# A hybrid SSD and attention encoder: dt in the exponents, a beginning in written order, and the gated norm chunk by chunk with its channel weights in the output weights

## Chip, cores and metric

The kernel runs on one core of one Trainium2 chip (the chip has eight). The metric is the device time of one execution in microseconds, the median of several runs. The core has a tensor engine (PE; its weight loads are PEld), a vector engine (DVE), a scalar engine (ACT), GpSimd (POOL) and a queue engine (SP); each goes through its own instructions in order and waits on semaphores of the others.

## What is computed

Two layers on x of 512 tokens by 1024 channels, then a final norm. Of a layer, shortened:

```python
h = rms_norm(x, norm1_w[i]); proj = h @ w_in[i]
z, xbc, dt_raw, q, k, v = split(proj)
xs, bm, cm = split(silu(depthwise_conv7(xbc)))
dt = softplus(dt_raw + dt_bias[i]); a = -exp(a_log[i])
y = ssd(xs, dt_fwd, a_fwd, bm, cm) + flip(ssd(flip(xs), flip(dt_bwd), ...)) + d_skip[i] * xs
y_ssm = rms_norm(y * silu(z), ssm_norm_w[i])     # per group of 512 channels
y_attn = windowed_gqa(q, k, v, sink, bias)       # |i-j| <= 128
x = x + concat(y_ssm, y_attn) @ w_out[i]
h = rms_norm(x, norm2_w[i]); g, u = split(h @ w_up[i])
x = x + (silu(depthwise_conv3(g)) * u) @ w_down[i]
```

ssd works in chunks of 128 tokens. Inside a chunk the output is a product with the matrix (C B^T) * exp(cum[l] - cum[s]) * dt[s], for s <= l forward and s >= l backward; across chunks a state is passed on, with 16 heads of 64 channels in two groups of eight heads.

## The kernel before

Everything is one program of some 20,000 instructions, four token tiles of 128 rows. A scheduler of the framework orders the instructions of each engine by priority and estimated times; the side work below is spread by hand.

**Weights.** Each product with weights is made in three parts: a block of weights is loaded raw by SP (prep_raw, L140), ACT casts it to a high part (whi, L152) and DVE subtracts to get the low part (wlo, L153, both in prep_split). mm3 (L263 to L265) then makes the three products with the activations, which are split the same way. Three raw and three split blocks are in flight.

**Beginning.** load_x0 (L226) loads the token tiles in halves, norm_weight (L216) loads the norm weight broadcast to 128 rows (512 KB). norm_token makes two Squares with a row sum on ACT (L287), the reciprocal root on POOL (L289, L290), one half of the product with the weight on DVE (L299) and the other on ACT and POOL (L301, L302); eight 128-column transposes on PE follow (L310), then a cast to the high part on ACT (L313) and the low part on DVE (L314). The bias table of attention is made by one product (L418), written to DRAM and spread into four Toeplitz arrays. The first product with weights is vdt: v and dt of all tokens, 96 products over 288 columns in layer 0. Then setup makes 42 small transposes of channel parameters (L256), dt_step makes softplus by a series on DVE (L483 to L498), six cumulative sums on PE (L511), their Exp on ACT (ex, L512), copies of the running sums (run, L515), their transposes (L518) and the write to DRAM (sums).

**State-space part.** Per group, bc_turn makes C B^T per chunk and two masked copies of it on DVE, cbf and cbb. ssd_steps returns a list of steps that Side.run spreads over the products with weights: over z (g_z) for the first group, over the output product (g_out) for the second. A unit u is four heads of a chunk, eight units per group. fetch loads the running sums as rows (POOL queue), build makes cbf * dt_fwd on ACT (L817) and adds cbb * dt_bwd on DVE (L818), decay subtracts each token's own sum on DVE (L828), takes the minimum of the two directions (L832), Exp on ACT (L833) and the product with build's result (L834, em). inner multiplies em with x on PE (L843). states passes the chunk states on (L785 to L794), outer adds the part from the states and d_skip * x (L855 to L866), multiplies by silu(z) and sums squares on ACT (L867).

**Gated norm.** After the last chunk, scale makes one reciprocal root for all four chunks (L274) and scales each on ACT (L873). turn then transposes by channel block j, all four chunks (L883), and applies the channel weight nprm in the cast (ACT, L884) and in the low part (DVE, L885). The output product reads mixS: group 0 in the last two weight blocks of each half (o0, o1), group 1 in token_outer (o2).

## Time and profile before

| | us |
|---|---|
| three runs: lowest, median, highest | 1574.24, 1574.35, 1574.81 |
| the profiled execution | 1572.24 |
| its span, first to last instruction | 1570.5 |
| PE busy / weight loads / DVE / ACT / POOL | 1518.9 / 1242.4 / 936.9 / 780.1 / 186.3 |
| mean granted clock of PE | 0.993 |

The rows further down come from one profiled execution. A row of a timeline has the start from the span's first instruction, the length, engine, line, operation, written and read tile, count, and in brackets the idle time before with what ended it. A row of a group has the count, the busy time, the mean of one in ns, and the idle time of the engine ahead of it. Tile names are the program's; many tiles share the name t (split activations) or pd and psm (PSUM banks).

### The profile page before, as it was taken

What the parts mean: (1) busy time and instruction counts of PE and PEld (TensorE: products, weight loads), DVE (VectorE), ACT (ScalarE), POOL (GpSimd) and SP (SyncE); (2) the same over time, 40 slices, a digit from 0 to 9 for tenths busy, and PEclk for the clock granted to TensorE, in tenths of its full rate; (3) what the DMA queues carried; (4) which work ended last, traced back from release to release, by engine and by line L of the source; (5) the groups of instructions that cost most, each with busy time, mean ns of one, the idle gap of its engine ahead of it and who ended that gap; (6) DMA issues with size and microseconds to landing.
All of it is one profiled execution on the core that took longest, in us unless ns stands there. A gap on an engine that the chain in (4) does not pass through costs nothing.

```text
span 1570.5 us, 20117 instructions
## 1 busy us (share of the span) xinstructions
PE 1518.9 (97%) x7676; PEld 1242.4 (79%) x7676; DVE 936.9 (60%) x1494; ACT 780.1 (50%) x1378; POOL 186.3 (12%) x226
## 2 busy tenths in 40 slices
PE   5999999999999999999999999989999999999997
PEld 5887778878788888888788777877778888888886
DVE  3776778996544444433367677799946444444333
ACT  4577886752543233322355789877335323332223
POOL 4000003433200000000010000043322000000002
PEclk9999999999999999999999999999999999999999
DMA  8432333553233333333343222336422323333221
GB/s 248 116 88 77 92 94 95 149 148 90 80 98 95 106 96 95 94 95 94 97 135 113 77 75 74 95 97 186 123 93 81 94 94 99 103 94 94 94 94 67
DMA packets 113796, 162.00 MB, mean 103 GB/s; under 512 B 8010, under 2 KB 90186, under 8 KB 113692
## 3 DMA queue, kind: packets, MB, share of 16 engines
q1 hardware_dynamic: 105476, 133.12, 27.8%
q0 software_dynamic: 7648, 27.50, 7.0%
q8 instruction: 60, 0.98, 0.3%
q14 instruction: 36, 0.29, 0.1%
q10 hardware_dynamic: 576, 0.10, 0.0%
HBM read 156.34 MB, written 8.55 MB: 105 GB/s over the span
## 4 chain that ended last, share of the span: by engine, by line
PE 81%; DVE 9%; issue 3%; ACT 3%; POOL 2%; DMA 1%; POOLq 0%; DVEq 0%; ACTq 0%
PE pd L263 21%; PE pd L264 20%; PE pd L265 20%; PE psm L263 3%; PE psm L264 3%; PE psm L265 3%; PE psm L608 2%; PE psm L598 2%; DVE dd L818 2%; DVE wlo L153 2%; PE psm L564 1%; ACT whi L152 1%; PE psm L565 1%; DVE rows L828 1%; PE psm L843 1%
## 5 line engine op out<-in xcount | busy, mean ns | idle before, releaser
L153 DVE TENSOR_TENSOR wlo<-raw,whi 128x1024 fp32r<-128x1024 f32 (+1 forms) x230 | 282.1, 1230 | 267.6 <-ACT whi L152 266.2
L263 PE MATMUL pd<-t,whi 128*128 128x512 f32 (+1 forms) x1088 | 419.0, 386 | 0.0
L265 PE MATMUL pd<-t,wlo 128*128 128x512 f32 (+1 forms) x1088 | 418.6, 385 | 0.4 <-DVE wlo L153 0.4
L264 PE MATMUL pd<-t,whi 128*128 128x512 f32 (+1 forms) x1088 | 418.0, 384 | 0.0
L152 ACT CAST whi<-raw 128x1024 fp32r<-128x1024 f32 (+1 forms) x230 | 238.5, 1041 | 263.9 <-PE pd L264 207.1
L265 PEld LDWEIGHTS pd<-t,wlo 128*128 128x128 f32 x1088 | 204.4, 188 | 40.3 <-DVE wlo L153 1.6
L263 PEld LDWEIGHTS pd<-t,whi 128*128 128x128 f32 x1088 | 204.2, 188 | 39.7 <-issue 1.9
L264 PEld LDWEIGHTS pd<-t,whi 128*128 128x128 f32 x1088 | 204.5, 188 | 39.1 <-issue 1.5
L263 PE MATMUL pd<-whi,t 128*128 128x256 f32 (+2 forms) x544 | 190.9, 351 | 0.6 <-ACT t L884 0.5
L264 PE MATMUL pd<-wlo,t 128*128 128x256 f32 (+2 forms) x544 | 182.8, 336 | 0.4 <-DVE wlo L153 0.2
L265 PE MATMUL pd<-whi,t 128*128 128x256 f32 (+2 forms) x544 | 181.8, 335 | 0.0
L263 PEld LDWEIGHTS pd<-whi,t 128*128 128x128 f32 x544 | 106.2, 195 | 13.7 <-issue 3.3
L264 PEld LDWEIGHTS pd<-wlo,t 128*128 128x128 f32 x544 | 106.2, 195 | 13.3 <-issue 3.8
L265 PEld LDWEIGHTS pd<-whi,t 128*128 128x128 f32 x544 | 105.6, 194 | 9.5 <-issue 0.6
L1026 DVE TENSOR_TENSOR pl<-t,ph 128x512 fp32r<-128x512 f32 x40 | 27.7, 692 | 119.4 <-ACT ph L1025 119.4
L1025 ACT CAST ph<-t 128x512 fp32r<-128x512 f32 x40 | 24.8, 620 | 147.7 <-PE psm L264 137.2
L360 DVE SCALAR_TENSOR_TENSOR sg<-pd,fprm,sg 128x511 f32<-128x511 f32 x88 | 65.9, 749 | 30.7 <-ACT sg L354 29.0
L566 DVE CUSTOM_DVE_ANT_0 s<-psm,bias,sink_all 128x256 f32<-128x256 f32 (+1 forms) x128 | 65.5, 548 | 22.8 <-PE psm L565 10.3
L580 ACT ACTIVATE s<-s,nm 128x257 f32<-128x257 f32 (+1 forms) x128 | 70.6, 556 | 2.6 <-DVE nm L577 2.5
L360 DVE SCALAR_TENSOR_TENSOR xT<-pd,cprm,xT 128x511 f32<-128x511 f32 (+2 forms) x96 | 66.9, 743 | 5.8 <-ACT xT L354 3.8
L263 PE MATMUL pd<-whi,ph 128*128 128x512 f32 x176 | 69.7, 396 | 0.0
L264 PE MATMUL pd<-wlo,ph 128*128 128x512 f32 x176 | 69.6, 396 | 0.0
(186 smaller groups left out, 2210.0 us busy)
## 6 DMA issues: line engine op xcount, KB each, us to landing
raw<-in_w_up_dram SPq DMA_DIRECT2D x88, 512.0 KB, 3.5
raw<-in_w_in_dram SPq DMA_DIRECT2D x52, 512.0 KB, 4.0
raw<-in_w_down_dram SPq DMA_DIRECT2D x44, 512.0 KB, 3.5
rows<-sums POOLq DMA_DIRECT2D x32, 512.0 KB, 5.7
raw<-in_w_out_dram SPq DMA_DIRECT2D x32, 512.0 KB, 4.2
bias<-toep POOLq DMA_DIRECT2D x16, 384.0 KB, 3.8
raw<-in_w_in_dram SPq DMA_DIRECT2D x18, 256.0 KB, 3.4
toep<-table POOLq DMA_DIRECT2D x4, 1024.0 KB, 9.5
```

The costliest lines, as they stand in the source:

```text
L152: S.copy(hi[:, :used], raw[:, :used])
L153: V.tensor_tensor(lo[:, :used], raw[:, :used], f(hi[:, :used]), ALU.subtract)
L263: mm(o, lh, rh, start=start, stop=False)
L264: mm(o, lh, rl, start=False, stop=False)
L265: mm(o, ll, rh, start=False, stop=stop)
L360: V.scalar_tensor_tensor(dst[:, lo:hi], src[:, lo + d : hi + d], taps[k], dst[:, lo:hi], ALU.mult, ALU.add)
L566: V.tensor_tensor_reduce(out=s4[:, h, :w], in0=ps[:, :w], in1=it.bias[h // 2][:, h % 2, it.j0 : it.j1], scale=1.0, scalar=sink4[:, h : h + 1],
L580: S.activation(s4[:, h, : w + 1], s4[:, h, : w + 1], AF.Exp, bias=nm4[:, h : h + 1], accum_out=den[:, h : h + 1])
L598: turn128(ps[:, c : c + P], it.s4[:, h, b * P : (b + 1) * P], ident)
L608: mm(po[c * HD : (c + 1) * HD, :256], v_sb[:, it.k0 // P + b, it.g * HD : (it.g + 1) * HD], it.pts[b][:, c * 256 : (c + 1) * 256], start=( ...
L818: V.scalar_tensor_tensor(dd[:, hs], cbb[:, cs], dts[:, c, 16 + hh + h : 17 + hh + h], dd[:, hs], ALU.mult, ALU.add)
L1026: V.tensor_tensor(l, p_sb[kt], f(h), ALU.subtract)
```

## The change

Four things. (1) dt goes into the exponents: dt_step makes ln(dt) with one Newton step after Ln and Exp, and own = ln(dt) - running sum; decay adds own of the backward direction on ACT (Identity with bias), copies it over the forward rows where the mask says s > l (a predicated copy on DVE), takes Exp with own of the forward direction as bias on ACT, and multiplies by the unmasked C B^T. build and the masked copies go; the backward direction's diagonal goes into skf, the factor of x in outer. (2) In layer 0 everything up to the end of vdt is in written order; the norm weight comes as one row of 4 KB and is spread by two products with ones; each token tile is one transfer, its norm one Square and two DVE products; the bias table comes behind the first vdt products. (3) The gated norm gets a reciprocal root per chunk, DVE scales the chunk, and turn transposes a chunk's four channel blocks. (4) The channel weights go into the split of those w_out blocks that multiply the state-space channels.

```diff
-            S.copy(hi[:, :used], raw[:, :used])
-            V.tensor_tensor(lo[:, :used], raw[:, :used], f(hi[:, :used]), ALU.subtract)
+            if key in scaled:
...
+                n = used // len(scaled[key])
+                for k, col in enumerate(scaled[key]):
+                    ks, wcol = slice(k * n, (k + 1) * n), nprm[:, col, key[0] : key[0] + 1]
+                    S.activation(hi[:, ks], raw[:, ks], AF.Copy, scale=wcol)
+                    V.scalar_tensor_tensor(lo[:, ks], raw[:, ks], wcol, f(hi[:, ks]), ALU.mult, ALU.subtract)
+            else:
+                S.copy(hi[:, :used], raw[:, :used])
+                V.tensor_tensor(lo[:, :used], raw[:, :used], f(hi[:, :used]), ALU.subtract)
...
                 add_unit((i, f"o{half}", j), wo, kt0, 2, [(512 * half, 512)])
+                if j >= 4:
+                    scaled[i, f"o{half}", j] = (kt0, kt0 + 1)
         for j in range(4):
             add_unit((i, "o2", j), wo, 4 + j, 1, [(0, 1024)])
+            scaled[i, "o2", j] = (4 + j,)
...
+    start = ExitStack()
+    start.enter_context(tc.manual_schedule())
...
-    load_x0(0)
-    wb0 = norm_weight(npool0, norm1_w[0])
+    wrow = npool0.tile([1, D], F32, name="wrow")
+    nc.scalar.dma_start(wrow, norm1_w[0:1])
+    nc.sync.dma_start(x_sb[0], x_in[0:P])
     prep_raw(1)
-    load_x0(1)
+    nc.sync.dma_start(x_sb[1], x_in[P : 2 * P])
...
+    wb0 = npool0.tile([P, D], F32, name="wb0")
+    for b in range(2):
+        psw = small_bank()
+        mm(psw, ones[0:1], wrow[:, 512 * b : 512 * b + 512], start=True, stop=True)
+        V.tensor_copy(wb0[:, 512 * b : 512 * b + 512], psw)
...
+    def first_norm(t):
+        xn = npool0.tile([P, D], F32, tag="xn", name=nm("xn"), bufs=2)
+        ss = smp.tile([P, 1], F32, tag="ss1", name=nm("ss"))
+        S.activation(xn, x_sb[t], AF.Square, scale=1.0 / 32.0, accum_out=ss)
+        rs = smp.tile([P, 1], F32, tag="rs1", name=nm("rs"))
+        G.tensor_scalar(rs, ss, EPS, None, ALU.add)
+        G.tensor_tensor(rs, rs, mhalf, ALU.pow)
+        yield
+        for b in range(2):
+            cs = slice(512 * b, 512 * b + 512)
+            V.scalar_tensor_tensor(xn[:, cs], x_sb[t][:, cs], rs, wb0[:, cs], ALU.mult, ALU.mult)
+        yield
+        for b in range(2):
+            turn_split(xn, t, b, hT)
+        yield
+    def turn_split(xn, t, b, dst):
...
+            if i == 0:
+                norms = [first_norm(t) for t in range(NT)]
+                next(norms[0])
+                next(norms[0])
+                prep_split(1)
+                next(norms[0])
+                next(norms[1])
+                next(norms[1])
+                prep_split(2)
+                next(norms[1])
+                next(norms[2])
+                next(norms[2])
+                prep_split(3)
+                vw = [splits.pop((i, "vdt", j)) for j in range(3)]
+                vdt(0, 0)
+                vdt(1, 0)
+                vdt(0, 1)
+                next(norms[2])
+                next(norms[3])
+                next(norms[3])
+                vdt(1, 1)
+                vdt(0, 2)
+                vdt(1, 2)
+                prep_raw(WBUF + RBUF)
+                bias_table()
+                next(norms[3])
+                for t in (2, 3):
+                    for j in range(3):
+                        vdt(t, j)
+                S.activation(expa_all, alog_all, AF.Exp)
+                start.close()
+            else:
+                vw = [take((i, "vdt", j)) for j in range(3)]
+                for t, j in ((t, j) for t in range(NT) for j in range(3)):
+                    vdt(t, j)
...
+                V.tensor_scalar(sp_w, dts, 1e-37, None, ALU.max)
+                S.activation(sp_a, sp_w, AF.Ln)
+                S.activation(sp_w2, sp_a, AF.Exp, scale=-1.0)
+                V.tensor_tensor(sp_w, sp_w, sp_w2, ALU.mult)
+                V.scalar_tensor_tensor(sp_a, sp_w, -1.0, sp_a, ALU.add, ALU.add)
...
+                V.tensor_tensor(
+                    own.rearrange("p c d h -> p c (d h)"), sp_a, run.rearrange("p c d h -> p c (d h)"), ALU.subtract
+                )
+                V.tensor_tensor(own[:, :, 1], own[:, :, 1], own[:, :, 0], ALU.subtract)
...
-                    cbf = ep.tile([P, L], F32, tag="cbf", name=nm("cbf"), bufs=2)
-                    cbb = ep.tile([P, L], F32, tag="cbb", name=nm("cbb"), bufs=2)
+                    cb = ep.tile([P, L], F32, tag="cb", name=nm("cb"), bufs=2)
...
-                    pv = ps.rearrange("p (c l) -> p c l", c=NT)
-                    for dst, m in ((cbf, t_le), (cbb, t_ge)):
-                        V.tensor_tensor(
-                            dst.rearrange("p (c l) -> p c l", c=NT),
-                            pv,
-                            f(m).unsqueeze(1).broadcast_to([P, NT, P]),
-                            ALU.mult,
+                    S.copy(cb, ps)
...
+                        V.scalar_tensor_tensor(
+                            junk, ps[:, sl], 1.0, ident, ALU.mult, ALU.mult, accum_out=own_cb[:, c : c + 1]
                         )
-                    r.update(bk=bk, cbf=cbf, cbb=cbb)
+                    skf = ep.tile([P, NT, GH], F32, tag="skf", name=nm("skf"), bufs=2)
+                    V.tensor_tensor(skf, dts[:, :, 16 + GH * g : 16 + GH * g + GH], bc_last(own_cb, GH), ALU.mult)
...
-                def build(u):
-                    c, hh = u // 2, h0 + 4 * (u % 2)
-                    dd = s2("dd", 3)
-                    cs = slice(c * P, (c + 1) * P)
-                    for h in range(4):
-                        hs = slice(h * P, (h + 1) * P)
-                        S.mul(dd[:, hs], cbf[:, cs], dts[:, c, hh + h : hh + h + 1])
-                        V.scalar_tensor_tensor(
-                            dd[:, hs], cbb[:, cs], dts[:, c, 16 + hh + h : 17 + hh + h], dd[:, hs], ALU.mult, ALU.add
-                        )
-                    dcb[u] = dd
-
                 def decay(u):
-
-
                     c, hh = u // 2, h0 + 4 * (u % 2)
                     rw = rows.pop(u)
+                    for h in range(4):
+                        S.activation(rw[:, 1, h], rw[:, 1, h], AF.Identity, bias=own[:, c, 1, hh + h : hh + h + 1])
+                    V.copy_predicated(rw[:, 0], behind.unsqueeze(1).broadcast_to([P, 4, P]), rw[:, 1])
+                    for h in range(4):
+                        S.activation(rw[:, 0, h], rw[:, 0, h], AF.Exp, bias=own[:, c, 0, hh + h : hh + h + 1])
+                    em = s2("em", 3)
                     V.tensor_tensor(
-                        rw, rw, run[:, c, :, hh : hh + 4].unsqueeze(3).broadcast_to([P, 2, 4, P]), ALU.subtract
+                        v4(em), rw[:, 0], cb[:, c * P : (c + 1) * P].unsqueeze(1).broadcast_to([P, 4, P]), ALU.mult
                     )
-                    em = s2("em", 3)
-                    V.tensor_tensor(v4(em), rw[:, 0], rw[:, 1], ALU.min)
-                    S.activation(em, em, AF.Exp)
-                    V.tensor_tensor(em, em, dcb[u], ALU.mult)
                     ems[u] = em
...
-                    G.tensor_tensor(v3(y), v3(xk[:, c]), bc_last(skip_all[:, 16 * i + h0 : 16 * i + h0 + GH], HD), ALU.mult)
+                    G.tensor_tensor(v3(y), v3(xk[:, c]), bc_last(skf[:, c], HD), ALU.mult)
...
-                    S.activation(y, sz[:, c], AF.Square, accum_out=ss[:, c : c + 1])
-
-                def scale():
-                    rs = rstd_of(ss, 512, NT)
+                    ss = smp.tile([P, 1], F32, tag="gss", name=nm("gss"))
+                    S.activation(y, sz[:, c], AF.Square, accum_out=ss)
+                    rss[c] = rstd_of(ss, 512)
+                rss = {}
+                def turn(c):
                     sz = r["sz"]
-                    for c in range(NT):
-                        S.mul(sz[:, c], sz[:, c], rs[:, c : c + 1])
-                    mixS[g] = (act_tile(), act_tile())
-
-                def turn(js):
-                    oh_, ol_ = mixS[g]
-                    sz = r["sz"]
-                    for j in js:
-                        wcol = nprm[:, 4 * g + j, i : i + 1]
-                        ps = small_bank()
-                        for c in range(NT):
-                            turn128(ps[:, c * P : (c + 1) * P], sz[:, c, j * P : (j + 1) * P], ident)
-                        S.activation(oh_[:, j], ps, AF.Copy, scale=wcol)
-                        V.scalar_tensor_tensor(ol_[:, j], ps, wcol, f(oh_[:, j]), ALU.mult, ALU.subtract)
+                    if mixS[g] is None:
+                        mixS[g] = (act_tile(), act_tile())
+                    V.tensor_scalar(sz[:, c], sz[:, c], rss[c], None, ALU.mult)
+                    ps = small_bank()
+                    pv = ps.rearrange("p (k c) -> p k c", k=4)
+                    for j in range(4):
+                        turn128(pv[:, j], sz[:, c, j * P : (j + 1) * P], ident)
+                    h, l = (m[:, :, c * P : (c + 1) * P] for m in mixS[g])
+                    S.copy(h, pv)
+                    V.tensor_tensor(l, pv, f(h), ALU.subtract)
...
-                    if k in range(8):
-                        build(k)
-
-                steps = [lambda k=k: step(k) for k in range(-1, 10)]
-                steps.append(scale)
-                steps += [lambda: turn((0, 1)), lambda: turn((2, 3))]
-                return steps
+                return [lambda k=k: step(k) for k in range(-1, 10)] + [lambda c=c: turn(c) for c in range(NT)]
```

The order of PE in layer 0 after vdt. Before, the small transposes (ident, with crow, frow, nrow) and the sums of dt (sp_e with the triangles) stand among products of the next projection (pd_678):

```order
L265 MATMUL pd_678<-t_9_116,wlo_600 128x512
L263 MATMUL pd_678<-t_9_116,whi_599 128x512
L256 MATMUL psm_460<-ident,nrow 128x2 x8
L511 MATMUL psm_493<-sp_e_471,t_le 128x64
L511 MATMUL psm_493<-sp_e_471,t_gt 128x64
L511 MATMUL psm_493<-sp_e_471,t_ge 128x64
L511 MATMUL psm_493<-sp_e_471,t_lt 128x64
L511 MATMUL psm_493<-sp_e_471,ones 128x64 x2
L264 MATMUL pd_678<-t_10_117,whi_599 128x512
L265 MATMUL pd_678<-t_9_116,wlo_600 128x512
L263 MATMUL pd_678<-t_9_116,whi_599 128x512
```

In the change the same stretch, from the last products of vdt (pd_190) to the first of the k projection (pd_514):

```order
L279 MATMUL pd_190<-wlo_252,t_12_123 128x288
L280 MATMUL pd_190<-whi_251,t_13_124 128x288
L271 MATMUL psm_409<-ident,crow 128x16 x12
L271 MATMUL psm_423<-ident,frow 128x8 x22
L271 MATMUL psm_447<-ident,nrow 128x2 x8
L581 MATMUL psm_481<-sp_e_459,t_le 128x64
L581 MATMUL psm_481<-sp_e_459,t_gt 128x64
L581 MATMUL psm_481<-sp_e_459,t_ge 128x64
L581 MATMUL psm_481<-sp_e_459,t_lt 128x64
L581 MATMUL psm_481<-sp_e_459,ones 128x64 x2
L278 MATMUL pd_514<-t_10_121,whi_516 128x512
L599 MATMUL psm_498<-ident,run_185 32x128 x4
```

The transposes, the sums and the running sums' transposes now follow vdt directly, and the next projection comes after them.

The order of ACT at the same place in the change; whi_516 is the high part of the first weight block of the k projection:

```order
L505 COPY v_177<-pd_190 128x256
L537 ACTIVATE expa_all<-alog_all 128x64
L554 ACTIVATE sp_e_459<-sp_e_459 128x128
L586 ACT_TABLE_LOAD
L586 ACTIVATE sp_a_462<-sp_w_460 128x128
L587 ACT_TABLE_LOAD
L587 ACTIVATE sp_w_60_461<-sp_a_462 128x128
L582 ACTIVATE ex_180<-psm_481 128x384
L161 CAST whi_516<-raw_329 128x1024
L592 COPY run_185<-psm_481 128x4x16 x2
L161 CAST whi_520<-raw_331 128x1024
```

That split now stands behind Ln, two Exps and two table loads; before, three splits stood ahead of the Exp of sp_e.

The order of DVE in the first group's state-space stretch of layer 0. Before, some one and a half units:

```order
L828 TENSOR_TENSOR rows_2605<-rows_2605,run_276 128x1024
L864 TENSOR_TENSOR y_2715<-y_2715,psm_2621 128x512
L832 TENSOR_TENSOR em_2742<-rows_2605 128x512
L866 TENSOR_TENSOR t_459_2389<-t_459_2389,y_2715 128x512
L818 SCALAR_TENSOR_TENSOR dd_2746<-cbb_859,dts_277,dd_2746 128x128 x4
L828 TENSOR_TENSOR rows_2690<-rows_2690,run_276 128x1024
L834 TENSOR_TENSOR em_2742<-em_2742,dd_2725 128x512
L832 TENSOR_TENSOR em_2825<-rows_2690 128x512
```

In the change, a like piece:

```order
L875 TENSOR_TENSOR xf_4501<-t_424_2171,sd_181 128x512
L939 TENSOR_TENSOR yo_2735<-psm_2733,ex_180 128x512
L911 TENSOR_TENSOR em_2729<-rows_2531,cb_864 128x512
L907 COPY_PREDICATED rows_2618<-t_gt,rows_2618 128x512
L941 TENSOR_TENSOR y_2731<-y_2731,psm_2634 128x512
L907 COPY_PREDICATED rows_2700<-t_gt,rows_2700 128x512
L943 TENSOR_TENSOR t_470_2414<-t_470_2414,y_2731 128x512
L911 TENSOR_TENSOR em_2762<-rows_2618,cb_864 128x512
```

Of a unit there remain a predicated copy and one product.

## Rows read from the trace of the kernel before

**Rows 1.** Page, its head: span, then busy time per engine with share and instructions.

```profile
span 1570.5 us, 20117 instructions
PE 1518.9 (97%) x7676; PEld 1242.4 (79%) x7676; DVE 936.9 (60%) x1494; ACT 780.1 (50%) x1378; POOL 186.3 (12%) x226
```

**Rows 2.** Stretches: length, busy us of PE, PEld, DVE, ACT, POOL; clock; DMA share; GB/s.

```profile
246.08:307.08 61.00, 56.25 (x378) 48.30 (x377) 58.98 (x87) 44.58 (x85) 27.68 (x22) 0.94 0.52 123
307.08:322.00 14.92, 13.88 (x67) 10.81 (x65) 14.75 (x21) 9.35 (x15) 6.16 (x5) 1.00 0.73 250
...
394.70:401.10 6.40, 3.24 (x17) 2.39 (x16) 1.93 (x3) 4.25 (x7) 1.23 (x2) 0.84 0.28 91
1017.70:1077.10 59.40, 53.34 (x361) 46.91 (x359) 58.06 (x83) 44.16 (x79) 24.02 (x22) 0.94 0.44 117
1165.30:1171.40 6.10, 2.63 (x18) 1.71 (x17) 1.97 (x3) 4.29 (x7) 1.23 (x2) 1.00 0.31 113
...
920.00:960.00 40.00, 40.00 (x237) 30.48 (x236) 29.61 (x79) 37.28 (x81) 3.80 (x9) 1.00 0.28 79
```

**Rows 3.** Waits of PE: line and its releaser; total us, times, longest.

```profile
PE psm L883 <- ACT t L873: 7.9, 11, 2.1
PE psm L843 <- DVE em L834: 7.3, 6, 1.7
```

**Rows 4.** Groups by line and shape, 246 to 307 us, ACT, then DVE.

```profile
L817 ACT ACTIVATE dd<-cbf,dts 128x128 f32<-128x128 f32 x41 | 13.3, 391 | 5.9 <-DVE em L834 5.9
L152 ACT CAST whi<-raw 128x1024 fp32r<-128x1024 f32 x7 | 7.3, 1039 | 2.2 <-PE pd L265 2.2
L833 ACT ACT_TABLE_LOAD x5 | 6.4, 1283 | 0.1
L833 ACT ACTIVATE em<-em 128x512 f32<-128x512 f32 x8 | 5.1, 632 | 7.4 <-DVE em L832 7.4
...
L818 DVE SCALAR_TENSOR_TENSOR dd<-cbb,dts,dd 128x128 f32<-128x128 f32 x34 | 16.8, 541 | 0.0
L828 DVE TENSOR_TENSOR rows<-rows,run 128x1024 f32<-128x1024 f32 x8 | 10.6, 1323 | 0.0
L153 DVE TENSOR_TENSOR wlo<-raw,whi 128x1024 fp32r<-128x1024 f32 x7 | 8.5, 1217 | 0.6 <-ACT whi L152 0.6
L832 DVE TENSOR_TENSOR em<-rows 128x512 f32<-128x512 f32 x8 | 7.4, 923 | 0.0
```

**Rows 5.** Timeline of PE, 0 to 40 us: start, length, instruction, idle before.

```profile
10.96 1.88 PE L418 MATMUL psm<-oh,rb 32*32 32x512 f32 x2 [10.96 <-DMA oh<-in_onehot_dram]
15.53 1.11 PE L310 MATMUL psm<-ident,xn 128*128 128x128 f32 x4 [2.69 <-DVE xn L299]
...
22.34 0.59 PE L263 MATMUL pd<-whi,t 128*128 128x288 f32 x1
...
39.22 0.40 PE L263 MATMUL pd<-t,whi 128*128 128x512 f32 x1
```

**Rows 6.** Timeline, 0 to 26 us: ACT, POOL, DVE.

```profile
6.18 0.63 ACT L287 ACTIVATE xn<-x 128x512 f32<-128x512 f32 x1 [0.26 <-DMA x<-in_x_dram]
21.57 2.04 ACT L313 CAST t<-psm 128x512 fp32r<-128x512 f32 x4
...
14.12 1.10 POOL L290 TENSOR_TENSOR rs<-rs,mhalf 128x1 f32<-128x1 f32 x2
...
14.72 1.41 DVE L299 SCALAR_TENSOR_TENSOR xn<-x,rs,wb 128x512 f32<-128x512 f32 x2 [1.21 <-POOL rs L290]
```

**Rows 7.** DVE timeline, 42 to 49 us; then PE busy in lines L256 and L511.

```profile
42.18 0.18 DVE L472 TENSOR_TENSOR xdt<-pd,dtb_all 128x32 f32<-128x32 f32 x1
48.16 0.29 DVE L498 SCALAR_TENSOR_TENSOR sp_e<-dts,expa_all 128x128 f32<-128x128 f32 x1
...
39.00:76.00 37.00, 3.09 (x42) 2.82 (x42) 1.00 0.42 113
...
39.00:76.00 37.00, 1.55 (x12) 1.41 (x12) 1.00 0.42 113
```

71 lines of the change are left out of this document (39 added, 32 removed).

## The prediction

> **What bounds the kernel now.** I read the head of the page first: the span is 1570.5 us and PE is busy for 97% of it [rows 1], so a change pays only where PE waits, or where it runs at the lower clock because it has just waited. The page leaves 51.6 us of the span in which PE is not busy. The table of stretches says where they lie. In the first head group's state-space stretch (from the first state product to the last inner product) PE is busy 56.25 of 61.00 us in layer 0 and 53.34 of 59.40 us in layer 1, and the granted clock is 0.94 in both (a mean over the two levels, 2.4 and 1.2 GHz: it falls to the lower one after a wait). Where the gated norm of the second group is turned, PE is busy 3.24 of 6.40 us and 2.63 of 6.10 us [rows 2]. The table of waits names the releasers: the turn L883 waits 7.9 us for the ACT scaling L873, and the inner product L843 waits 7.3 us for the DVE product L834 [rows 3]. The rest is the beginning: the first transpose starts at 15.53 us and the first product with weights at 22.34 us [rows 5].
>
> In the state-space stretch DVE is the engine that ends last: busy 58.98 of 61.00 us, against 44.58 us for ACT [rows 2]. Of it the combined mask products (L818) are 16.8 us, the subtraction over 1024 columns (L828) 10.6 us and the minimum (L832) 7.4 us [rows 4].
>
> **State-space stretch, first group.** Per unit (eight per group) the change takes from DVE four L818, one L828 and one L832, and adds one predicated copy over 512 columns. From ACT it takes four L817 and the 512-column Exp, and adds eight ACTIVATEs over 128 columns. DVE loses 16.8 + 10.6 + 7.4 = 34.8 us. The predicated copy is nowhere in this trace: at least the 512-column L832 (0.92 us), at most the 1024-column L828 (1.32 us), since it writes half as much; I take 0.92, as the width is the same. Eight of them and four rescalings of about 0.8 us leave DVE at 58.98 - 34.8 + 7.4 + 3 = 35 us. It no longer binds. ACT: 13.3 us for 41 L817 is 0.324 each, so 64 x 0.324 = 20.8 us come and 32 x 0.324 + 5.1 = 15.5 us go, and ACT has 44.6 + 5.3 = 49.9 us [rows 4]. What PE itself needs is 61.00 less 4.75 idle and less what the clock cost (6% of 61.00 = 3.7 us): 52.6 us; in layer 1 it is 59.40 - 6.06 - 3.6 = 49.7 us [rows 2]. So ACT, with 49.9 us and every step in order, is now as full as PE. A unit crosses ACT, DVE, ACT, DVE instead of DVE, ACT, DVE, and in the change's order some of its Exps stand behind a Silu that waits for PE, while two DVE products stand behind a sum from POOL. At most 8.4 and 9.7 us can come back, at least nothing. I take a little over half: 4.5 and 5.0 us, together **-9.5 us**.
>
> **Gated norm by chunk.** Now four ACT scalings follow one rstd over all four chunks, and no turn can start before them. The change scales a chunk on DVE as soon as its own rstd is there, and the order puts the first group's turns between blocks of 24 products. That stretch, 14.92 us long, has 1.04 us idle, and the four scalings make PE wait between the turns too; I take 1.5 us a layer, bounds 0 and 2. In the second group PE still turns all 16 in one piece after 24 products, but only the last chunk can be late. PE idles 3.16 and 3.47 us there now, and its clock is 0.84 in layer 0 [rows 2]. I take 3.7 us a layer, bounds 2 and 4.5, since the last chunk's chain of DVE, POOL and ACT is no longer than those 24 products and the first 12 transposes; late next is the split of the next weight block, on DVE before the turned chunks. Together **-3.0 and -7.4 us**.
>
> **The channel weights** move into the split of eight weight blocks a layer. Four become two ACTIVATEs and two DVE operations over 512 columns: some 0.3 us more on either engine each. The rest keep their sizes. In those stretches ACT and DVE have slack once the mask work is gone, so I cost it at nothing; without that cover it would be 8 x 0.3 = 2.4 us. The single-chunk rstds add three pairs on POOL per group, hidden beside its 27.68 busy of 61.00 us [rows 2].
>
> **Attention stage.** DVE loses two masked products per group and gains four 128-column ones and two small ones, about even. ACT gains one 512-column copy per group, four in all at 0.6 us. In layer 1 ACT is busy 37.28 of 40.00 us there [rows 2]. Between 0 and 2.4 us; I take **+0.8 us**.
>
> **The beginning.** Now the first token tile is normalized only after 512 KB of broadcast norm weight, on ACT, POOL and DVE with two POOL products; PE's first weight product starts at 22.34 us and the 96 of them end where the next projection begins, at 39.22 us: 16.9 us, with 16 transposes among them [rows 5]. In the change the tiles run one behind the other, since ACT makes a tile's two casts before the next tile's Square. One tile is: Square 1.2 us, rstd 0.9 (half of the pair's 1.10 and its sum before), DVE 0.7 + 0.7, second turn 1.1 at the low clock, cast 0.5 [rows 5, 6]: 5.1 us. Tile 0 can start at 6.2, where the second half of it is read now [rows 6]. The weight row has then to go through two products like L418 (1.88 us) and two copies, which holds tile 0 back by about a microsecond, and tile 1 is turned at about 17.1 us. From there PE has the same 96 products and 16 transposes as now, 16.9 us, and the bias product of 0.9 us: it is through at 35 us instead of 39.2. That is **-4.2 us**; bounds 0 (late tiles 2 and 3) and 6 us. SP issues the four tiles as one transfer each and no longer has blocks of the next projection, which wait for buffers, ahead of the last one. POOL sends out the bias table and the four Toeplitz writes later than now; what reads them comes only with the attention stage, so I cost that at nothing, and a first attention step that waited for them would cost PE a few us.
>
> **What stands behind it.** Now the 42 setup transposes and the dt sums lie between products of the next projection, so the chain of dt is covered. In the change's order PE goes from the last of the 96 straight to the transposes, then to the dt sums, and only then to the next projection; ACT makes that projection's first split after Ln, Exp and the chunk exponentials. So from 35 us on: 12 transposes 0.9 (of 3.09 for 42) and a copy 0.3, the DVE chain 42.18 to 48.45 = 6.3, the clamp 0.3, Ln 0.4, table load 1.28, Exp 0.4, Exp of the sums 0.5, split 1.04 and 1.22 [rows 4, 7]: 12.6 us. PE has 3.09 + 1.55 + 0.6 = 5.2 us of work in it [rows 7] and is idle for 7.4 us. After such a wait the clock falls; I add 1.8 us, half of what it cost in 61 us of the state-space stretch. **+9.2 us**, bounds 3 (if the split gets in earlier) and 12. Nothing covers it, and every engine's queue is behind it. Layer 1 keeps its order on PE; the Ln and its loads delay ACT by some 2.4 us there, and four dense products cover part: **+0.7**, bounds 0 and 2.4.
>
> The change's ACT order has two table loads in that chain, one before Ln and one before Exp, of 1283 ns each in this profile [rows 4]. The Trainium skill, ScalarE: Activation LUTs, section on table sets, says that one set holds both Ln and Exp and that the pair needs one load. By that rule the stall would be 1.3 us shorter; the order as built has both, so the sum has both.
>
> **Sum** against the profiled execution, 1572.24 us: -9.5 - 3.0 - 7.4 + 0.8 - 4.2 + 9.2 + 0.7 = -13.4, so 1558.8. The median of the runs shown is 2.1 us above that execution; against it the forecast is **1561 us**.
>
> **Rivals.** (1) All waits of PE in the state-space stretch go: -18.1 instead of -9.5, 1552 us. With the stall of the beginning at its lower bound, 1546. For it speaks that DVE is 97% busy now and falls to 35 us; against it that ACT is then as full as PE. Chance 0.2. (2) ACT takes DVE's place, and the kernel gets slower. ACT idles 61.00 - 44.58 = 16.4 us in that stretch now, mostly waiting for DVE [rows 2, 4]. Each unit still waits for DVE between its two groups of ACTIVATEs. If these waits stay as long, the stretch takes 49.9 + 16.4 = 66.3 us, 5.3 us more than now, in both layers: +10.6 instead of -9.5, 1581 us. It decides from some 13 us of idle ACT on. Against it: only half as long a DVE step stands between, and DVE is free. Chance 0.1. The Trainium skill, ScalarE: Activation LUTs, rules for kernel authors, tells to put additions and products on VectorE and not on ScalarE; this change does the reverse with four additions a unit, and the rule would come out as this rival. (3) The two halves cancel: the stall reaches 12 us, the beginning gains nothing, and the stretch gives 4 us: about 1572, no change. Chance 0.08.
>
> **Chances and range.** The forecast has 0.62; rival 1 has 0.2, on the same side. A measurement of this kernel can tell 0.2% (3 us) from no change. Faster 0.82, same 0.08, slower 0.10. From 1546 (rival 1 with the short stall) to 1573 (rival 3), about 1 in 6 is left out.
>
> **What would show it.** Right: the first product with weights near 17 us; after the 96th a hole in PE of 4 us before the dt sums and one of about 3 us before the next projection; no L873 among PE's waits; DVE under 45 us and ACT near 50 us in the stretch, which takes some 56 us. Wrong: PE continuous from 17 to 60 us, ACT with long waits for the predicated copy, or a predicated copy over 1.4 us.

## The result, and the profile after

The changed kernel takes 1551.18 us (median of 4 runs, 1549.04 to 1552.18) against 1574.3 us for the kernel before: a ratio of 0.9851, interval 0.9839 to 0.9863. The profiled execution took 1550.66 us, 21.6 us less than that of before. The forecast was 1561 us: right in sign and range, 10 us too high.

The head of the page, to be held against [rows 1]:

```profile
span 1549.0 us, 20219 instructions
PE 1508.9 (97%) x7680; PEld 1238.0 (80%) x7680; DVE 876.5 (57%) x1406; ACT 793.4 (51%) x1464; POOL 174.7 (11%) x246
```

DVE lost 60 us of work, ACT gained 13, and PE is busy for the same 97% of the span. The gain has to be looked for stage by stage. The table of stretches (columns as in [rows 2]): the first group's state-space stretch of layer 0, the stretch behind it with the turns, the same two of layer 1.

```profile
248.65:304.91 56.26, 52.30 (x374) 45.69 (x372) 41.62 (x48) 48.62 (x100) 26.30 (x28) 1.00 0.47 122
304.91:323.66 18.75, 18.75 (x91) 15.45 (x90) 16.44 (x24) 16.02 (x36) 4.00 (x5) 1.00 0.77 241
...
1007.24:1063.43 56.19, 52.30 (x373) 45.69 (x372) 41.61 (x48) 48.61 (x100) 26.28 (x28) 1.00 0.48 123
1063.43:1082.00 18.57, 18.57 (x91) 15.27 (x89) 16.26 (x24) 16.02 (x36) 3.82 (x5) 1.00 0.68 236
```

The stretch is 4.7 and 3.2 us shorter. It does not hold the same products as before (in layer 0 it holds 0.6 us less of them, in layer 1 some 1.5 us more); at equal work, by PE's lag as explained below, it gained 4.2 and 4.7 us. DVE has 41.6 us of work where it had 59, and behind it PE has no gap left. The clock does not fall in it in this execution (0.94 before). That is not so in each: in two runs further down with the same instructions in this stretch (the changed kernel with shifted tiles and that with another rounding) it falls once in either layer, and the stretch takes 57.3 to 57.6 us, here layer 0 of the shifted one:

```profile
247.85:305.18 57.33, 53.79 (x373) 47.20 (x372) 41.56 (x48) 48.61 (x100) 26.27 (x28) 0.97 0.43 121
```

So the stretch of one execution can be read to 1.1 to 1.4 us only. PE's waits of the whole execution (line, releaser; total us, times, longest), against [rows 3]:

```profile
PE psm L314 <- DVE xn L303: 4.9, 2, 3.5
PE psm L581 <- DVE sp_w L585: 4.9, 1, 4.9
PE pd L279 <- DVE wlo L162: 3.9, 2, 2.0
PE psm L922 <- DVE em L911: 3.0, 4, 1.2
...
PE psm L599 <- ACT run L592: 1.7, 1, 1.7
...
PE pd L278 <- ACT whi L161: 1.5, 1, 1.5
```

The 7.9 us for the ACT scaling of the gated norm are gone, the 7.3 us for the mask product are 3.0 us for the new one. New are a wait of 4.9 us of the dt sums (L581) and 1.5 us of the next projection behind them: the uncovered dt chain.

To put a number on each stage I took PE's start times and subtracted, for every instruction, what the ones before it take back to back (per kind of product, the lower quartile of its starts' distances in the kernel before). What is left is PE's lag: waits and low clock. Both kernels do the same products, so lags compare at equal work (us):

```
at the start of                     before   after   stage's change   forecast
what follows the 96 vdt products      20.1    12.6        -7.5          -4.2
first attention score, layer 0        21.4    23.1        +9.1          +9.2
first state product, layer 0          29.1    30.7        -0.1          +0.4
second group's first state product    41.7    37.3        -6.0          -6.0
what follows the second norm's turns  51.6    43.1        -4.1          -3.7
layer 1's first turn                  54.3    43.1        -2.7           0
first attention score, layer 1        58.1    48.7        +1.8          +0.7
first state product, layer 1          66.1    56.8         0.0          +0.4
second group's first state product    78.9    63.4        -6.2          -6.5
what follows the second norm's turns  88.8    69.7        -3.5          -3.7
the last product                      91.6    69.6        -2.9           0
```

The column of the forecast spreads the prediction's terms over the same stages; it adds up to -13.4, the measured one to -22.0. Two stages make the difference: the beginning, and the MLP of both layers (-2.7 and -2.9), in which the change touches nothing.

### The profile page after: what moved, and what is told of

Its sections match the earlier page's. It is cut to its first block, busy times and chain, and to the rows that moved or that the text cites. A ratio compares the mean times of both kernels' runs of the same rounds, so it can differ in the third digit from the quotient of the medians.

```text
span 1549.0 us, 20219 instructions
## 1 busy us (share of the span) xinstructions
PE 1508.9 (97%) x7680; PEld 1238.0 (80%) x7680; DVE 876.5 (57%) x1406; ACT 793.4 (51%) x1464; POOL 174.7 (11%) x246
## 4 chain that ended last, share of the span: by engine, by line
PE 86%; ACT 4%; DVE 3%; issue 3%; POOL 2%; DMA 2%; POOLq 0%; ACTq 0%; DVEq 0%
PE pd L280 22%; PE pd L278 22%; PE pd L279 22%; PE psm L278 3%; PE psm L279 3%; PE psm L280 3%; PE psm L690 2%; PE psm L680 2%; PE psm L922 1%; PE psm L646 1%; DMA rows<-sums 1%; PE psm L647 1%; PE psm L937 1%; ACT whi L161 1%; PE psm L314 1%
## 5 line engine op out<-in xcount | busy, mean ns | idle before, releaser
L162 DVE TENSOR_TENSOR wlo<-raw,whi 128x1024 fp32r<-128x1024 f32 (+1 forms) x214 | 260.5, 1221 | 241.3 <-ACT whi L161 241.0
L161 ACT CAST whi<-raw 128x1024 fp32r<-128x1024 f32 (+1 forms) x214 | 221.8, 1040 | 240.9 <-PE pd L279 213.6
L278 PEld LDWEIGHTS pd<-whi,t 128*128 128x128 f32 x544 | 103.9, 191 | 13.7 <-issue 3.8
L280 PEld LDWEIGHTS pd<-whi,t 128*128 128x128 f32 x544 | 103.8, 191 | 11.5 <-DVE t L962 1.6
```

What stands on the lines that cost most here:

```text
L161: S.copy(hi[:, :used], raw[:, :used])
L162: V.tensor_tensor(lo[:, :used], raw[:, :used], f(hi[:, :used]), ALU.subtract)
L278: mm(o, lh, rh, start=start, stop=False)
L280: mm(o, ll, rh, start=False, stop=stop)
```

## Experiments

### The MLP: place of the tiles, rounding

In the MLP's down projection PE works without a gap in both kernels, yet it is faster after. ph and pl are the high and the low part of its activations. One group of the products over ph, of the kernel before, then of the change:

```profile
L263 PE MATMUL pd<-whi,ph 128*128 128x512 f32 x176 | 69.7, 396 | 0.0
```

```profile
L278 PE MATMUL pd<-whi,ph 128*128 128x512 f32 x176 | 68.9, 391 | 0.0
```

On average one of the products over ph and pl starts 0.233 us after the one before it in the kernel before, and 0.228 us in the change (in the median 0.232 and 0.227); over 1056 products that is the 2.7 and 2.9 us of lag, 5.6 together. The change makes later tiles lie 128 bytes higher, so I moved them, in both kernels.

```
+    spare = cp.tile([P, 32], F32, name="spare")
+    G.memset(spare, 0.0)
```

> The kernel before with one unused 128-byte tile ahead of the other tiles, so that every later tile (ph and pl among them) lies 128 bytes higher, as in the change; no other instruction but one POOL memset. Theory placement: the down-projection products over ph and pl start every 0.233 us in the kernel before and every 0.227 us in the changed one, 1056 of them, and this is so because of where the tiles lie; then this run shows their mean at 390 ns instead of 395 ns and is 5 to 6 us faster, 1568 to 1569 us. Rival chip or run: the difference belongs to the execution and not to the code; then 395 ns stays, or falls in the run of the kernel before as well, and the time is 1574 us.

> The changed kernel with the same unused 128-byte tile, so that ph and pl lie 256 bytes above their place in the kernel before. Theory placement, repeating every 256 bytes: the products over ph and pl fall back to 395 ns and the time is 5 to 6 us longer, 1556 to 1557 us. Rival placement, peculiar to the place in the kernel before: 390 ns stays and the time is 1551 us. Rival chip or run: no change, 1551 us.

Measured: the shifted kernel before 1573.92 us (ratio 0.9999, 0.999 to 1.0009), its products at 395 to 397 ns; the shifted changed kernel 1549.36 us (0.985, 0.9836 to 0.9863), at 390 to 392. A shift by 128 bytes does not matter, and the difference stayed with the code in a second execution of either. Last, the values:

```
-            V.scalar_tensor_tensor(xn[:, cs], x_sb[t][:, cs], rs, wb0[:, cs], ALU.mult, ALU.mult)
+            V.scalar_tensor_tensor(xn[:, cs], wb0[:, cs], rs, x_sb[t][:, cs], ALU.mult, ALU.mult)
```

> The changed kernel with two operands of one DVE product exchanged in the first norm: (weight x rstd) x token instead of (token x rstd) x weight. Nothing else differs, neither an instruction's place nor its length; only the last bits of the activations do. It asks what sets the 390 or 395 ns of the down-projection products over ph and pl: so far the changed kernel and all of its variants whose values should be the same to the last bit have 390, the kernel before and all three undone ones, which round otherwise, have 395; neither the tiles' place, nor their order, nor the number of instructions sorts them so. Theory values: 395 ns, 1556 to 1557 us. Rival: the values do not matter, 390 ns, 1551 us, and the cause stays open.

1550.52 us (0.9852, 0.9832 to 0.9872), 389 to 391 ns: a change in the last bits of the values does not do it either. All fourteen kernels of this document fall in one of two modes in their traced executions. The kernel before (shifted or not) and the three kernels below that undo one part of the change have 394 to 397 ns, all others 389 to 392; both modes were measured on one and the same chip. Undoing any one part brings the slower mode back, so no one part alone carries the difference, and **the cause is open**. For the rest it matters that an undone part costs 5.6 us that are not its own.

### Undoing one part each

**The exponents.** The decay, the mask products, the dt step and the skip weights of the kernel before, in the changed kernel:

```
-                    for h in range(4):
-                        S.activation(rw[:, 1, h], rw[:, 1, h], AF.Identity, bias=own[:, c, 1, hh + h : hh + h + 1])
-                    V.copy_predicated(rw[:, 0], behind.unsqueeze(1).broadcast_to([P, 4, P]), rw[:, 1])
...
+                    V.tensor_tensor(
+                        rw, rw, run[:, c, :, hh : hh + 4].unsqueeze(3).broadcast_to([P, 2, 4, P]), ALU.subtract
+                    )
```

> The changed kernel with dt taken out of the exponents again: the mask products, the subtraction, the minimum and the one Exp of the kernel before stand in the state-space stretch and in the dt step; beginning, gated norm and weights as in the change. Theory: in the first group's stretch the change took 4.7 us in layer 0 and 4.2 in layer 1 (61.00 to 56.26, 59.40 to 55.16), because DVE ended last there; undone, the stretches are back at 60 to 61 and 59 us with DVE over 55 us busy, and the time is 1560 us. Rival: the turns by chunk between the products gave the gain there, DVE was only busy, not late; then the time is 1552 us. The products over ph and pl, 390 ns in the change and 395 before: if the exponents carry that difference, 395 ns and 5 to 6 us more come back here, 1565 us.

1569.01 us (0.9965, 0.9952 to 0.9978), 17.8 us slower than the change; 12.2 without the MLP. Its first group's stretches in layer 0 and 1:

```profile
252.09:314.06 61.97, 54.91 (x361) 48.48 (x359) 58.96 (x84) 44.59 (x80) 28.93 (x28) 0.92 0.48 119
1018.15:1078.78 60.63, 53.65 (x360) 47.09 (x359) 58.63 (x84) 44.45 (x80) 28.77 (x27) 0.94 0.45 122
```

And its waits of PE:

```profile
PE psm L914 <- DVE em L905: 11.0, 6, 2.6
PE psm L580 <- DVE sp_e L567: 5.1, 2, 4.9
```

The stretch is back at 62.0 and 60.6 us with DVE over 58 us busy and the clock at 0.92 and 0.94, and PE's wait for the mask product (L914, 11.0 us) is longer than in the kernel before (7.3 us) [rows 3]: the theory, with 3 us more than it gave. So the exponents carry the gain of this stretch, and with the mask work in it DVE is the engine that ends last. The turns by chunk, the rival, do not carry it: they are in this run. The dt chain stays open without Ln too (4.9 us).

**The gated norm and the folded weights.**

```
-                return [lambda k=k: step(k) for k in range(-1, 10)] + [lambda c=c: turn(c) for c in range(NT)]
+                steps = [lambda k=k: step(k) for k in range(-1, 10)]
+                steps.append(scale)
+                steps += [lambda: turn((0, 1)), lambda: turn((2, 3))]
+                return steps
...
-            scaled[i, "o2", j] = (4 + j,)
```

> The changed kernel with the gated norm of the kernel before: one rstd over four chunks, four ACT scalings, 16 turns in two steps, the channel weights at the turned tiles and no scaled weight splits. Theory: the chunks took 4.1 and 3.5 us in the second group and 1.3 and 2.0 us behind the first group's stretch, together 10.9 us; undone, 1561 to 1562 us, with PE waiting 6 to 8 us for the ACT scaling again. Rival: with DVE free the four scalings come early anyway and half of it stays, 1556 us. If the norm carries the 390 ns of the products over ph and pl, 5 to 6 us more.

1580.34 us (1.0041, 1.0027 to 1.0055): slower than the kernel before. It is 29.2 us over the change, 23.6 without the MLP, where I expected 10.9. The waits of PE:

```profile
PE psm L959 <- ACT t L949: 9.6, 12, 2.1
PE psm L877 <- DVE xf L872: 6.6, 2, 4.4
```

Besides the 9.6 us for the four scalings, a state product early in the second group waits 4.4 and 2.3 us for a DVE product, where the longest such wait in the kernel before is 1.8 us, and in the traced execution the clock falls six times between the beginning and the end, in that of the change never. In lag, the second group alone is 11.6 and 8.3 us worse than in the change. The first group's stretch, with the exponents in it but without the turns by chunk, is even 1.5 us shorter than in the change:

```profile
248.55:303.30 54.75, 52.13 (x374) 45.67 (x372) 38.33 (x46) 48.56 (x100) 24.04 (x22) 1.00 0.47 127
```

So the two parts are not additive. The three undone kernels (the beginning follows) lose 12.2, 23.6 and -5.7 us with the MLP taken out, 30.1 together; the change gained 17.5 without it. That ACT is the reason, which has both the additions of the exponents and the scalings of the old norm here, fits the rows, but no run separates it. The exponents alone, without the written beginning, were not run.

**The beginning.**

```
-    wrow = npool0.tile([1, D], F32, name="wrow")
-    nc.scalar.dma_start(wrow, norm1_w[0:1])
...
+    load_x0(0)
+    wb0 = norm_weight(npool0, norm1_w[0])
```

> The changed kernel with the beginning of the kernel before: no written order, norm weight by one broadcast transfer, tiles of x in two halves, the bias table at the start. Theory: at equal work done the beginning gives 7.5 us up to the last of the 96 vdt products and the uncovered dt chain takes 9.1 us behind them, so the two together cost 1.6 us; undone, 1549 to 1550 us, with the first product near 22 us and no wait of PE before the dt sums. Rival: the beginning pays for itself, the chain of dt would be open here as well (Ln and its table loads are new); then 1555 to 1558 us. If the beginning carries the 390 ns of the products over ph and pl, 5 to 6 us more.

1551.11 us (0.9854, 0.9835 to 0.9873), the same as the change; the MLP taken out, it is 5.7 us faster. PE's lag at the first attention score is 19.2 us against 23.1: the written beginning is 5.2 us ahead at the end of the vdt products and gives back 9.1 behind them. With the old beginning the dt chain is covered, with Ln in it. The written beginning as built does not pay; the theory holds, by more than it said: 3.9 us of the 5.7 stand in these lags.

### The uncovered chain

What stands in it in the change, PE first (timeline: start, length, instruction, idle before):

```profile
31.89 0.29 PE L280 MATMUL pd<-whi,t 128*128 128x288 f32 x1
...
34.24 0.63 PE L271 MATMUL psm<-ident,nrow 2*128 2x2 f32 x8
39.76 0.66 PE L581 MATMUL psm<-sp_e,t_le 128*128 128x64 f32 x2 [4.89 <-DVE sp_w L585]
...
41.49 1.06 PE L581 MATMUL psm<-sp_e,ones 128*128 128x64 f32 x4
44.06 0.79 PE L278 MATMUL pd<-t,whi 128*128 128x512 f32 x1 [1.51 <-ACT whi L161]
```

ACT in the same stretch:

```profile
34.21 1.28 ACT L586 ACT_TABLE_LOAD   x1
...
40.11 1.28 ACT L587 ACT_TABLE_LOAD   x1
...
42.59 0.49 ACT L582 ACTIVATE ex<-psm 128x384 f32<-128x384 f32 x1 [0.87 <-PE psm L581]
42.97 1.04 ACT L161 CAST whi<-raw 128x1024 fp32r<-128x1024 f32 x1
```

From the last of the 96 products to the next projection's first are 12.0 us (forecast 12.6), in which PE stands still for 4.89 and 1.51 us; the clock is at its lower level from 35.2 to 48.9 us. Three attempts to cover it. First only the text: k's projection written ahead of the dt step.

```
+            side.run(g_ws((i, "k"), hT, k_done), 0)
             dt_step()
             dtx.close()
...
-            side.run(g_ws((i, "k"), hT, k_done), 0)
```

> The changed kernel with the projection of k written ahead of the dt step in both layers, so that its 96 products can stand between the last of the 96 vdt products and the dt sums. Theory uncovered chain: the 4.9 and 1.5 us in which PE stands still and the 2.5 us that the lower clock costs after it go, and in layer 1 the 0.5 and 1.7 us too; 1551 less 8 to 10 is 1541 to 1543 us. Rival weights late: the splits of k cannot start before the vdt products free their buffers, PE waits for them instead, and half comes back at most, 1547 us. Rival order: the scheduler puts the dt sums ahead all the same, 1551 us.

1553.14 us (0.9868, 0.9854 to 0.9881), not to be told from the change: the rival on the order. PE still goes from the transposes to the sums (they start at 39.46 us). Then half of k in the written order:

```
+                        if t == 3 and j < 2:
+                            prep_split(4 + j)
...
+                setup()
+                next(kgen)
+                start.close()
```

> The changed kernel with the written order of the beginning drawn on through the first half of k's projection: its two weight splits behind the first and second third of the last tile's vdt products, then the 42 setup transposes, then 48 products, and the scheduler from there; so the dt sums stand behind these 48 products. Theory uncovered chain: the 6.4 us in which PE stands still and the 2.5 us at the lower clock go; 1551 less 8 to 9 is 1542 to 1543 us. Rival weights late: the splits, which need the buffers of the vdt products, come late and PE waits 3 to 5 us for them, 1546 to 1548 us. Rival moved wait: the dt chain now lies among the splits on DVE and ACT, and PE waits for the second half of k or for q instead; 1551 us.

1549.73 us (0.9845, 0.9825 to 0.9865), no gain: the rival on the moved wait. The sums stand behind 48 products now and still wait, longer than before, since the scheduler put a fourth weight split into the middle of the dt chain on DVE. That split waits for a buffer that k's products free. PE at the sums of this run:

```profile
54.98 0.69 PE L582 MATMUL psm<-sp_e,t_le 128*128 128x64 f32 x2 [5.85 <-DVE sp_e L569]
```

And its DVE, with the split between two steps of the chain:

```profile
38.78 0.29 DVE L559 TENSOR_TENSOR sp_w<-sp_w 128x128 f32<-128x128 f32 x1
49.11 1.23 DVE L162 TENSOR_TENSOR wlo<-raw,whi 128x1024 fp32r<-128x1024 f32 x1 [10.04 <-ACT whi L161]
50.25 0.22 DVE L560 TENSOR_SCALAR sp_a<-sp_w 128x128 f32<-128x128 f32 x1
```

So the dt step had to be in the written order as well, ahead of that split:

```
                 next(kgen)
+                dt = dt_step()
+                next(dt)
+                next(kgen)
+                next(dt)
                 start.close()
```

> As the run with the first half of k written, but the dt step is in the written order too: its whole DVE chain stands behind the first three weight splits and ahead of the fourth, its sums behind the 48 products of k's first half, and the second half of k stands between the sums and the four turns of the sums. Theory: the chain of 12 us then lies under k's 48 products (11 us) and PE waits nowhere for it; what the uncovered chain took in the changed kernel, 9.1 us up to the first attention score at equal work, falls to 2 us at most (the clock falls once behind the 42 short transposes), so 1551 less 7 is 1544 us. Rival: the wait moves on to the next weight split again, 1550 us. Apart from that the time stands 5.6 us higher if the products over ph and pl run at 395 ns instead of 390, as in the three undone kernels; that is read from their rows and taken out.

1546.47 us (0.9822, 0.9808 to 0.9837), 4.7 us under the change, whose interval begins at 0.9839. On PE's timeline the sums follow the 48 products without a gap, and k's second half follows them:

```profile
46.93 0.39 PE L278 MATMUL pd<-t,whi 128*128 128x512 f32 x1
47.16 0.33 PE L582 MATMUL psm<-sp_e,t_le 128*128 128x64 f32 x2
...
47.99 0.61 PE L582 MATMUL psm<-sp_e,ones 128*128 128x64 f32 x4
48.41 0.48 PE L278 MATMUL pd<-t,whi 128*128 128x512 f32 x1
```

The stage costs a lag of 5.2 us instead of 10.5; expected were 2 at most. One fall of the clock and waits of 0.7 and 2.0 us for the copies that free k's banks remain.

### What is left in the state-space stretch

PE still idles 3.96 and 3.89 us there. The groups of the change, ACT then DVE, 248 to 305 us:

```profile
L909 ACT ACTIVATE rows<-rows,own 128x128 f32<-128x128 f32 x32 | 10.8, 392 | 2.0 <-DVE rows L907 1.9
L906 ACT ACTIVATE rows<-rows,own 128x128 f32<-128x128 f32 x32 | 10.3, 391 | 3.0 <-DMA rows<-sums 3.0
L909 ACT ACT_TABLE_LOAD x6 | 7.7, 1283 | 0.0
L848 ACT ACT_TABLE_LOAD x6 | 7.7, 1283 | 0.1
...
L907 DVE COPY_PREDICATED rows<-t_gt,rows 128x512 f32<-128x512 int32 x8 | 8.0, 999 | 0.4 <-ACT rows L906 0.3
...
L955 DVE TENSOR_SCALAR t<-t,rs 128x512 f32<-128x512 f32 x2 | 3.8, 1918 | 2.8 <-POOL rs L289 2.8
```

All of this idle time ends with DVE: in either layer a weight split (1.95 us), two products em (L911, 1.5 us; they wait for ACT's Exp in their turn) and a state (0.4 to 0.5 us). ACT's additions on DVE, one instruction for four:

```
-                    for h in range(4):
-                        S.activation(rw[:, 1, h], rw[:, 1, h], AF.Identity, bias=own[:, c, 1, hh + h : hh + h + 1])
+                    V.tensor_tensor(
+                        rw[:, 1], rw[:, 1], own[:, c, 1, hh : hh + 4].unsqueeze(2).broadcast_to([P, 4, P]), ALU.add
+                    )
```

> The changed kernel with the four ACT additions of a unit (Identity, 128 columns each) replaced by one DVE addition over 512 columns. Theory ACT as full as PE: ACT loses 10.3 of 48.6 us in the first group's stretch and DVE gains 8 x 0.7 us; PE idles 4.0 us there, of which 1.5 us end with ACT's Exps and 2.0 with a weight split; 1 to 2 us come back in each layer, 1548 to 1549 us. Rival: every step in order, not ACT's fill, sets the waits, and DVE's queue is where they end; then 1551 us or more. Apart from that 5.6 us more if the products over ph and pl run at 395 ns.

1553.25 us (0.986, 0.9841 to 0.988): no gain, and 2 us that cannot be told from the change. In the stretch ACT falls from 48.6 to 42.5 us, and it gets no shorter:

```profile
248.65:307.84 59.19, 54.97 (x373) 48.39 (x372) 48.53 (x64) 42.47 (x77) 28.39 (x27) 0.94 0.46 127
1008.85:1066.47 57.62, 51.99 (x374) 45.41 (x372) 46.52 (x61) 40.72 (x75) 26.77 (x26) 1.00 0.48 129
```

The group of the new additions on DVE, 248 to 309 us:

```profile
L905 DVE TENSOR_TENSOR rows<-rows,own 128x512 f32<-128x512 f32 x11 | 8.6, 793 | 5.2 <-DMA rows<-sums 5.1
```

The addition is the step that waits for the rows' transfer (5.1 us); in DVE's queue everything else DVE owes to PE waits with it. PE idles 4.2 and 5.6 us in the stretch (4.0 and 3.9 in the change), so ACT's fill was not the limit. The stretches are 2.9 and 1.4 us longer than in the change, but only 1.9 and 0.0 us longer than in the changed kernel with shifted tiles, which has the change's instructions: that the additions on DVE cost time is not shown. The rule that additions belong on VectorE (the Trainium skill, ScalarE: Activation LUTs, rules for kernel authors) gained nothing here by these rows.

The weight split that PE waits for (1.95 us in each layer) stands behind the scaling L955, as DVE's timeline of the change shows:

```profile
278.76 3.35 DVE L955 TENSOR_SCALAR t<-t,rs 128x512 f32<-128x512 f32 x1
...
286.83 0.49 DVE L955 TENSOR_SCALAR t<-t,rs 128x512 f32<-128x512 f32 x1 [2.76 <-POOL rs L289]
287.23 2.35 DVE L162 TENSOR_TENSOR wlo<-raw,whi 128x1024 fp32r<-128x1024 f32 x2
```

On POOL, where the rstd is made:

```
-                    V.tensor_scalar(sz[:, c], sz[:, c], rss[c], None, ALU.mult)
+                    G.tensor_scalar(sz[:, c], sz[:, c], rss[c], None, ALU.mult)
```

> The changed kernel with the scaling of a chunk by its rstd on POOL, where the rstd is made, instead of DVE. Theory: on DVE this scaling stands in the queue for 2.8 us until POOL has the rstd, and once runs 3.35 us instead of 0.48 while POOL runs three products, and the weight split that PE waits for (1.95 us in either layer) stands behind it; without it that wait goes, and 2 us come back in each layer, 1547 us. Rival: the scaling takes over 1 us on POOL and the turns of the second group come later, 1551 us. Apart from that 5.6 us more if the products over ph and pl run at 395 ns.

1549.3 us (0.9844, 0.9825 to 0.9862). PE's wait for weight splits falls from 3.9 to 1.7 us, and 1.6 us of waits for POOL's scaling come in their place; a gain of 1.9 us lies inside the scatter: inconclusive. Both edits together:

> The run with the dt step written, and the scaling of a chunk on POOL as well. Theory: the two work in different places; of the 2.0 us in which PE waits for a weight split in either layer most go, and the waits of the turns for POOL (0.8 us each) take some of it back: 1546 less 1 to 3 is 1543 to 1545 us. Rival: the wait in the state-space stretch moves on to the decay products, as with the additions on DVE, and the time stays at 1546 us.

1545.65 us (0.9824, 0.9809 to 0.9838): not to be told from the dt step written alone. These two are the fastest kernels of the study, about 5 us under the change and 28 under the kernel before.

## Why the prediction was right, and by how much not

**State-space stretch (-9.5): right in what bound it and in size, not in why only half comes back.** At equal work it is -4.2 and -4.7 us, where 4.5 and 5.0 were taken (1.1 to 1.4 us less in an execution with a fall of the clock); undone, the time is back. The expectation of the first undone run has 55.16 us for the stretch of layer 1; that ends it 1 us before its last products are through, it takes 56.19. The prediction took a little over half since "ACT, with 49.9 us and every step in order, is now as full as PE". ACT has 48.6 us, but with 6 us less on it nothing came back, and in the run with the old gated norm the stretch is 1.5 us shorter with ACT as full. What remains are waits for DVE, so that just half came back is in part luck. DVE fell to 41.6 us, not 35, and the main reason is not one of the terms: the products that scale x for the states (xf) take 8.2 us in the stretch against 2.6, since eight of them lie in it and not four, and four of the eight take 1.17 to 1.55 us, all beside POOL instructions. DVE's groups for them, before and after:

```profile
L785 DVE TENSOR_TENSOR xf<-t,sd 128x512 f32<-128x512 f32 x4 | 2.6, 680 | 0.0
L875 DVE TENSOR_TENSOR xf<-t,sd 128x512 f32<-128x512 f32 x8 | 8.2, 1064 | 0.0
```

The scalings of chunks and the predicated copy (0.999 us on average, 0.72 to 1.85, bounds 0.92 and 1.32) are 1.4 us over their terms together.

**Gated norm (-3.0 and -7.4): right.** The stage of the first group less its stretch at equal work gives -1.8 and -1.5, the second group -4.1 and -3.5. What the prediction did not see is that the exponents need this part: with the exponents and the beginning alone the kernel is slower than before (1580 us). Less the 5.7 us of the beginning that is 1574.6, no gain.

**Attention (+0.8):** -0.1 and 0.0; the copies cost nothing.

**The beginning (-4.2): mis-sized, -7.5, outside its bound of 6.** The step that failed is "Tile 0 can start at 6.2, where the second half of it is read now". In the change tile 0 is one transfer, first in SP's queue, and its Square starts at 4.50 us. Nor did the weight row hold it back by a microsecond: its second copy ends at 6.8 us, 0.2 us after the rstd. ACT and DVE on the timeline of the change:

```profile
4.50 1.06 ACT L296 ACTIVATE xn<-x 128x1024 f32<-128x1024 f32 x1 [1.65 <-DMA x<-in_x_dram]
...
6.75 1.41 DVE L303 SCALAR_TENSOR_TENSOR xn<-x,rs,wb 128x512 f32<-128x512 f32 x2
```

From there the tiles come 5.4 us apart (5.1 forecast), the first product with weights starts at 14.61 us instead of the forecast 17.1, and it takes 17.5 us from there to the end of the 96, with the bias product (17.8 forecast).

The prediction also misread what held the first tile back in the kernel before. The wait that ended last was not that for the 512 KB of norm weight: DVE's first product waits for the rstd from POOL [rows 6], and on POOL tile 0's root stands behind tile 1's sum, for which POOL waits until ACT has made tile 1's Squares, behind a weight cast that waits 4.47 us for its transfer:

```profile
13.75 0.29 POOL L289 TENSOR_SCALAR rs<-ss 128x1 f32<-128x1 f32 x1 [6.44 <-ACT xn L287]
```

The written order puts each tile's root behind its own sum.

**The dt chain (+9.2): right, +9.1,** with 6.4 us of idle time (7.4 forecast) and more of low clock. The prediction says that its sum has both table loads; the 12.6 us hold one of 1.28 us. It made no difference: the first load lies in ACT's wait for DVE, the second beside PE's sums, and the Exp of the sums behind it still waits 0.87 us for PE. By the rule of the Trainium skill (ScalarE: Activation LUTs, table sets) one load would do; by these rows it would have saved nothing. **Layer 1 (+0.7):** +1.8, inside its bound of 2.4, with waits of 0.5 us for dt and 1.7 us for the copy of the sums.

**Not in the sum:** the MLP, -5.6 us. No term stood for it, and nothing in the diff points there.

The time came out at rival 1's 1552 us, but not by rival 1: the waits in the stretch did not all go (7.9 us of idle PE remain in the two layers). It was the forecast's case, with 3.3 us more from the beginning and 5.6 from the MLP; without the MLP the time would be 1556.8 us. Rival 2 did not come, and moving work from ACT back to DVE gained nothing: ACT's fill does not set the waits that are left.

## What to carry to other kernels

Write down a chain that crosses engines together with the work that covers it: a written order that ends ahead of the chain leaves it bare, and half of the cover only moves the wait to the next transfer of a buffer. Parts of a change that load the same engine are tried together and singly; here one of them without the other gained nothing. An engine's idle time is no room for a step that waits: what stands behind it in the queue waits too. Before a stretch of two kernels is compared by its length, see that it ends at the same product and holds the same work.

## What the runs showed of the hardware

The same 1056 products run at 0.233 or 0.228 us each on average, at one of the two in the traced execution of each of the fourteen kernels, with no wait and a granted clock of 1.00 in either; a shift of the tiles by 128 bytes or another rounding did not move a kernel from one to the other. DVE's TENSOR_SCALAR over 512 columns, 0.47 to 0.49 us else, took 3.35 us twice, each time beside three POOL products in a row. POOL's timeline at the first of them (278.76 to 282.11 us):

```profile
278.29 1.29 POOL L940 TENSOR_TENSOR y<-y,yo 128x512 f32<-128x512 f32 x1
...
279.53 1.04 POOL L932 TENSOR_TENSOR y<-t,skf 128x512 f32<-128x512 f32 x1
280.54 1.28 POOL L940 TENSOR_TENSOR y<-y,yo 128x512 f32<-128x512 f32 x1
```

The Trainium skill, SBUF — State Buffer, section Who interferes with whom, says that DVE and GpSimd share a pair of ports by an exclusive lock, and that a DVE instruction in a mode with two ports, which a tensor_scalar can enter, and a GpSimd instruction contend for it: the later one blocks fully. The rows agree for this instruction (3.06 of its 3.35 us lie beside POOL's, three in a row); in which mode it ran no run here shows.
